# Weight-sum pieces of a decoder block: one event each, loaded and half summed through GpSimd, with six additions made by DMA

## The chip, the cores and the metric

The kernel runs on one core of a Trainium2 chip. A core has five engines with instruction queues of their own: TensorE (PE in the profile; its weight loads are listed as PEld), VectorE (DVE), ScalarE (ACT), GpSimd (POOL) and SyncE (SP, which here only issues DMAs). Each engine works through its queue in order; an instruction that must wait holds everything behind it on its engine. DMAs can be issued from SP, ACT and POOL, and run on 16 shared DMA engines. The metric is the time of the core in microseconds (us), a median over runs.

## The reference

One layer of a hybrid decoder block on x of 2048 tokens by 1024, everything in float32:

```python
h = _rmsnorm(x, norm_pre_mix)
proj = einsum('bsd,de->bse', h, w_in)            # q, k, v, u, z and two gates
merged = (gate_a * einsum('bse,ed->bsd', y_attn, w_branch_attn)
          + gate_b * einsum('bse,ed->bsd', y_gmlp, w_branch_gmlp))
y = einsum('bsd,de->bse', merged, w_out)
x = x + _rmsnorm(y, norm_post_mix)

h = _rmsnorm(x, norm_pre_mlp)
a = relu(einsum('bsd,df->bsf', h, w_mlp_in))     # 1024 -> 4096
y = einsum('bsf,fd->bsd', a * a, w_mlp_out)      # 4096 -> 1024
x = x + _rmsnorm(y, norm_post_mlp)
```

`y_attn` is a dilated window attention and `y_gmlp` a chunked spatial gating; both are done before the part of the kernel that is of interest here.

## The kernel before

**Precision.** A float32 operand is split into a high part (rounded to float32r) and a low part (the rest). A product of two such operands is three matmuls (high by high, high by low, low by high; `mm3`, lines 95 to 98). Each moves 512 columns. `split` (line 68) makes the two parts: a copy, usually on ACT, and a subtraction, usually on DVE (line 79).

**Fewer products.** The MLP's first product (w_mlp_in by h) is done with a two-level Strassen scheme in Winograd's form: seven outer products instead of eight, each of seven inner ones. The price is sums of operand blocks. For the outer level these are four sums of the weight blocks (S1 to S4) and four of the activation blocks (T1 to T4). They are worked out ahead, as *pieces*, and kept in DRAM (`ws_d` for the weights, `t_d` and `tq_d` for the activations).

**Part 2** is the stretch from the gated merge to x + norm(y). It goes over four chunks of 512 tokens in the order 2, 3, 0, 1. For each chunk:

- `merge` (line 1194) has eight turns `dt`, each with 18 matmuls. A turn needs two gates: `load_gate` (line 1182) loads them through SP into a few buffers, `open_gate` applies the sigmoid on ACT (line 1191), DVE multiplies them with the matmuls' result (line 1208), adds the two (line 1210), and `split` makes the operand `mg`.
- `out_block` (line 1232) has four blocks `i` of 128 tokens, each with 48 matmuls. Afterwards ACT squares the result out of PSUM for the norm (line 1256), DVE multiplies it by the gain (line 1257), adds the residual tile `xr` that SP has loaded (lines 1237 and 1261), POOL's queue stores it (`x1_d`, line 1264), and DVE makes the normed `y1` (line 1266). PE transposes `y1` later, in the middle of a later block or merge (line 1271, called through `flush`), and POOL's queue stores the transposed rows (`h2_d`, line 1273). There is one `xr` tile: SP reloads it once the store of the block before has read it.

**The pieces of Part 2.** `w_piece(t)` (line 1304) loads two slices of w_mlp_in of 512 KB, tile `v` (tag `tr`, `trw` in the profile) and tile `w` (tag `tq`, `tqw`), makes four sums of 128 x 512 in place, all on DVE (lines 1313 to 1317), and stores the two tiles through POOL's queue (lines 1315 and 1318). `t_piece` (line 1288) does the same with rows of h2. There is one buffer for each tile, so a piece's loads wait until the stores of the one before have landed. Both are generators with three steps; the loads are issued by SP. `next_piece` (line 1326) runs the next step whenever it is called: once in each of the last four turns of the first merge, once or twice after each output block of the first three chunks, and once in each turn of the later merges. There are 13 weight pieces (`W_EARLY`) and two activation pieces.

**Who sets the order.** PE's order is as written. In Part 2 the order of the other four engines is made by a planner, when the program is built: it takes the instruction whose inputs it expects to be ready. `behind` (line 179) pins what is issued inside it behind the last instruction issued so far on each engine; it sets the earliest place, not the place. From line 1748 on, in the MLP, `as_written` makes all engines follow the program.

**The MLP's first product** has 56 steps of seven inner products, 392 products of six matmuls, numbered `k`. The work beside them is put on a list with `later(k, ...)`. `combine` (line 1381) makes a step's weight sums: POOL adds, ACT rounds, DVE subtracts. `hproduct` (line 1538) adds the products into sums X by DVE (lines 1564 and 1566). For the outer product M5 (fourth of the seven), each result `t` is added to X, by POOL for column half 1 and by DVE for half 0 (line 1570, run from line 1957), and stored to `m5_d`. Two more kinds of pieces are on the list: `outer_load`, `outer_sum`, `outer_store` (from line 1494; eight pieces, one DVE and one POOL sum each, at k = 4 + 5n), and `w_load`, `w_sum`, `w_store` (from line 1515; the 16 - 13 = 3 late weight pieces, two DVE and two POOL sums each, at k = 118 + 6n). These two share the ring buffers `c1` and `xs`, four tiles each, and load and store through SP.

Of the kernel before, what the change touches and what calls it, by code (L numbers as in the profile page):

```python
# [9 lines left out]
F32 = mybir.dt.float32  # L10
F32R = mybir.dt.float32r
AF = mybir.ActivationFunctionType
OP = mybir.AluOpType
# [4 lines left out]
P = 128  # L18
# [3 lines left out]
NF = 32  # L22
# [3 lines left out]
HALF = 1024  # L26
# [16 lines left out]
def block_kernel(ctx, tc, a, out):  # L43
    nc = tc.nc
    pe, act, dve, pool, sp = nc.tensor, nc.scalar, nc.vector, nc.gpsimd, nc.sync
# [101 lines left out]
    h2_d = dtile([P, KT, S], "h2d")  # L147
# [221 lines left out]
    with ExitStack() as e1a:  # L369
# [12 lines left out]
        p = psum_aux("busy")  # L382
# [27 lines left out]
        with as_written():  # L410
# [5 lines left out]
            p = psum_aux("busy")  # L416
# [868 lines left out]

    T_AT, WS_AT = ("T1", "T3", "T4", "T2"), ("S2", "S4", "S3", "S1")

    def t_piece(kk):

        w, v = (ttp.tile([P, 2, 512], F32, name=f"{n}{kk}", tag=n, bufs=1) for n in ("tq", "tr"))  # L1290
        for t, k in ((w, kk), (v, kk + 2)):
            sp.dma_start(t.rearrange("p c t -> p (c t)"), h2_d[:, k, HALF:])
        yield
        b11, b12, b21, b22 = w[:, 0], w[:, 1], v[:, 0], v[:, 1]
        dve.tensor_sub(b11, b12, b11)
        dve.tensor_sub(b12, b22, b12)
        pool.dma_start(t_d[:, kk, 0:2], w)
        yield
        dve.tensor_sub(b22, b22, b11)
        dve.tensor_sub(b21, b21, b22)  # L1300
        pool.dma_start(t_d[:, kk, 2:4], v)
        yield

    def w_piece(t):

        w, v = (ttp.tile([P, 2, 512], F32, name=f"{n}w{t}", tag=n, bufs=1) for n in ("tq", "tr"))
        sp.dma_start(v.rearrange("p a c -> p (a c)"), a["w_mlp_in"][t + NF // 2].rearrange("p k c -> p (k c)"))
        yield
        sp.dma_start(w.rearrange("p a c -> p (a c)"), a["w_mlp_in"][t].rearrange("p k c -> p (k c)"))
        yield  # L1310
        a11, a12, a21, a22 = w[:, 0], w[:, 1], v[:, 0], v[:, 1]
        q, f = divmod(t, 2)
        dve.tensor_add(a22, a21, a22)
        dve.tensor_sub(a21, a11, a21)
        pool.dma_start(ws_d[q][:, 2:4, f], v)
        dve.tensor_sub(a11, a22, a11)
        dve.tensor_sub(a12, a12, a11)
        pool.dma_start(ws_d[q][:, 0:2, f], w)
        yield
# [6 lines left out]
    def next_piece(_=None):  # L1326
        while True:
            if not piece:
                if not pieces:
                    return  # L1330
                piece.append(pieces.popleft())
            with behind():
                try:
                    return next(piece[0])
                except StopIteration:
                    piece.clear()

    chunks = (2, 3, 0, 1)
    e3 = ExitStack()
# [146 lines left out]
    def later(k, f, *args):  # L1486
        todo.setdefault(k, []).append((f, args))
# [50 lines left out]
    def hproduct(k, n, i):  # L1538

        o, q = hsteps[n]  # L1540
        m = OUTER[o][0]
        j, name = USE[i]
        which = {1: "a", 6: "a", 7: "a", 4: "a", 2: "b", 5: "c", 3: "c"}[i]
        if i in (1, 2, 5):
            bank_[n, which] = psum_any(f"h{which}_{n}")
        p = bank_[n, which]
        for kk in range(2):
            w, b = hs_[n], w2_[(o, kk), name]
            for z, (l, r) in enumerate(((0, 0), (0, 1), (1, 0))):
                pe.matmul(p, w[:, l, S_AT[i], kk * P:(kk + 1) * P], b[r], start=i in (1, 2, 5) and not kk and not z,  # L1550
                          stop=kk == 1 and z == 2, skip_group_check=True)
        f, c = PLACE[i]
        first, last_one = i in (1, 6, 7, 4), i in (2, 3, 4, 5)
        x_ = X[2 * q + f][:, c * 512:(c + 1) * 512]
        if m in (2, 3, 5):
            if first:
                stage_[n, f, c] = rx.tile([P, 512], F32, name=f"e{n}{f}{c}", tag="c1" if c else "xs", bufs=4)
            t = stage_[n, f, c]
        else:
            t = x_  # L1560
        if m in (1, 5) and first:
            act.activation(t, p, AF.Copy)
        elif m in (2, 3) and first:
            dve.tensor_add(t, x_, p)
        else:
            dve.tensor_add(t, t, p)  # L1566
# [53 lines left out]
    def spatial_out(dt):  # L1620

        nonlocal ttp, gpost, gmlp
        if dt < 2:
            sz_out(*late.pop(0))
        if dt == 1:
            ez.close()
            mgp.append(stack(e2, "mg1", 1))
            gxp.append(stack(egx, "gx", 1))
            ttp = stack(e2r, "ttp", 2, side="right")
            load_wo(2)  # L1630
            load_wo(3)
        split_wo(dt)
        if dt > 3:
            next_piece()
# [12 lines left out]
    ttp = None  # L1647
# [2 lines left out]
    mg = merge(2, yt, {}, spatial_out)  # L1650
    for n, c in enumerate(chunks):
        if n:
            mg = merge(c, yt, {0: flush, 2: flush}, next_piece)
        for i in range(4):
            b = out_block(c, i, mg, flush_older)
            next(b)
            last.append(b)
            for _ in range((1, 2, 2, 0)[n]):
                next_piece()
# [31 lines left out]
    assert not pieces  # L1691

    def load_w2(q):

# [365 lines left out]
```

## Time and profile before

| | us |
|---|---|
| median of three runs (2649.35 to 2654.46) | 2650.83 |
| the profiled run | 2654.96 |
| its span in the profile | 2653.2 |
| PE busy in the span | 2567.0 |
| DVE busy | 1852.8 |
| POOL busy | 1364.0 |
| ACT busy | 1106.2 |

The page's fourth part gives a chain that covers almost nothing here, so the stages are read one by one. By the stretch view, the span's stages are: projections and attention from 0 to about 1010 us, the last gating chunks to 1062, Part 2 from 1062 to 1436, the first MLP product to 2026, and the second MLP product to the end. A matmul's own row shows 389 ns, but matmuls overlap: what counts is the distance from one start to the next, and so the number of matmuls in a stretch. "PEclk" is the granted clock of TensorE as a share of full speed.

### The profile page before, as it was taken

What the parts mean: (1) busy time and instruction counts of PE and PEld (TensorE: products, weight loads), DVE (VectorE), ACT (ScalarE), POOL (GpSimd) and SP (SyncE); (2) the same over time, 40 slices, a digit from 0 to 9 for tenths busy, and PEclk for the clock granted to TensorE, in tenths of its full rate; (3) what the DMA queues carried; (4) which work ended last, traced back from release to release, by engine and by line L of the source; (5) the groups of instructions that cost most, each with busy time, mean ns of one, the idle gap of its engine ahead of it and who ended that gap; (6) DMA issues with size and microseconds to landing.
All of it is one profiled execution on the core that took longest, in us unless ns stands there. A gap on an engine that the chain in (4) does not pass through costs nothing. (4 is left out here: it accounts for less than half of the span.)

```text
span 2653.2 us, 35700 instructions
## 1 busy us (share of the span) xinstructions
PE 2567.0 (97%) x12122; PEld 2127.6 (80%) x12122; DVE 1852.8 (70%) x3187; ACT 1106.2 (42%) x2324; POOL 1364.0 (51%) x1265
## 2 busy tenths in 40 slices
PE   9999999999999999989889999999999999999998
PEld 8888888788888877777667887877777888888886
DVE  5676665535443456766667889999888887788867
ACT  5213111254455444454435522443234555555555
POOL 0363354374454554211123656766698677677634
PEclk9999999999999999999999999999999999999999
DMA  8879768988888899866776467446885221222235
GB/s 320 285 245 327 261 229 289 300 278 255 291 288 236 234 304 318 287 213 230 243 251 228 166 190 230 139 159 194 249 250 175 89 81 62 88 88 88 88 115 210
DMA packets 412136, 568.69 MB, mean 214 GB/s; under 512 B 58801, under 2 KB 247473, under 8 KB 410930
## 3 DMA queue, kind: packets, MB, share of 16 engines
q1 hardware_dynamic: 385872, 502.63, 58.4%
q0 software_dynamic: 16192, 57.16, 5.5%
q10 hardware_dynamic: 9890, 6.62, 0.8%
q8 instruction: 96, 1.57, 0.2%
q14 instruction: 86, 0.70, 0.1%
HBM read 362.16 MB, written 204.14 MB: 213 GB/s over the span
## 5 line engine op out<-in xcount | busy, mean ns | idle before, releaser
L1550 PE MATMUL ha<-spot,hs 128*128 128x512 f32 x1344 | 334.9, 396 | 27.5 <-DVE X_yt L1566 10.4
L1550 PEld LDWEIGHTS ha<-spot,hs 128*128 128x128 f32 x1344 | 252.1, 190 | 92.3 <-DVE X_yt L1566 10.7
L1859 PE MATMUL ya<-spot,s 128*128 128x512 f32 x1344 | 323.5, 389 | 2.3 <-DVE X_yt L1867 2.3
L1859 PEld LDWEIGHTS ya<-spot,s 128*128 128x128 f32 x1344 | 252.2, 188 | 55.3 <-issue 1.8
L1550 PE MATMUL hc<-spot,hs 128*128 128x512 f32 x672 | 173.7, 394 | 2.8 <-DVE e L1566 1.8
L728 PE MATMUL g<-opA,spots 128*128 128x512 f32 x672 | 170.8, 398 | 1.9 <-DVE cv L760 1.9
L1859 PE MATMUL yc<-spot,s 128*128 128x512 f32 x672 | 170.5, 389 | 0.0
L728 PE MATMUL g<-opB,spots 128*128 128x512 f32 x648 | 164.7, 398 | 0.3 <-DVE ga L766 0.3
L1550 PEld LDWEIGHTS hc<-spot,hs 128*128 128x128 f32 x672 | 127.3, 191 | 33.1 <-DVE e L1566 3.5
L96 PE MATMUL x<-hT_a,wq 128*128 128x512 f32 x384 | 149.7, 390 | 0.0
L98 PE MATMUL x<-hT_a,wq 128*128 128x512 f32 x384 | 149.4, 389 | 0.0
L97 PE MATMUL x<-hT_a,wq 128*128 128x512 f32 x384 | 149.4, 389 | 0.0
L1859 PEld LDWEIGHTS yc<-spot,s 128*128 128x128 f32 x672 | 126.2, 188 | 26.2
L728 PEld LDWEIGHTS g<-opA,spots 128*128 128x128 f32 x672 | 120.9, 188 | 24.2 <-issue 2.3
L79 POOL TENSOR_TENSOR spots<-gr,spots 128x512 fp32r<-128x512 f32 x98 | 127.9, 1309 | 23.7 <-DMA gr<-in_w_in_dram 9.4
L1723 ACT ACTIVATE sraw<-sraw 128x1024 f32<-128x1024 f32 x128 | 134.7, 1052 | 1.7
L79 POOL TENSOR_TENSOR spot<-w2r,spot 128x512 fp32r<-128x512 f32 x79 | 112.1, 1443 | 45.1 <-ACT spot L71 45.1
L728 PEld LDWEIGHTS g<-opB,spots 128*128 128x128 f32 x648 | 116.6, 188 | 22.3 <-POOL spots L73 0.7
L71 ACT ACTIVATE hl<-r 128x512 fp32r<-128x512 f32 x48 | 30.4, 633 | 236.5 <-POOL r L329 89.0
L978 DVE TENSOR_REDUCE o<-po 128x256 f32<-128x512 f32 x48 | 33.2, 692 | 132.1 <-PE po L977 132.1
L73 POOL TENSOR_SCALAR spots<-gr 128x512 fp32r<-128x512 f32 x86 | 55.4, 645 | 134.6 <-PE g L728 92.0
L96 PE MATMUL o<-wo,mg 128*128 128x512 f32 x256 | 101.9, 398 | 2.1 <-ACT mg L71 2.1
(460 smaller groups left out, 6801.6 us busy)
## 6 DMA issues: line engine op xcount, KB each, us to landing
sraw<-sd SPq DMA_DIRECT2D x128, 256.0 KB, 3.3
qk<-hl SPq DMA_DIRECT2D x24, 1024.0 KB, 5.7
qq<-qk SPq DMA_DIRECT2D x96, 256.0 KB, 5.3
sd<-e SPq DMA_DIRECT2D x64, 256.0 KB, 4.9
hraw<-wsd SPq DMA_DIRECT2D x32, 512.0 KB, 4.6
w2r<-in_w_mlp_out_dram SPq DMA_DIRECT2D x16, 1024.0 KB, 8.2
g<-gated SPq DMA_DIRECT2D x56, 256.0 KB, 5.9
gr<-sgd SPq DMA_DIRECT2D x53, 256.0 KB, 5.2
```

Of the source, the lines that this page charges most:

```text
L71: act.activation(hi, src, AF.Copy)
L73: pool.tensor_scalar(hi, src, 1.0, 1.0, op0=OP.mult, op1=OP.mult)
L79: (pool if lo_eng == "pool" else dve).tensor_sub(lo, src, f32(hi))
L96: pe.matmul(ps, lh, rh, start=start, stop=False)
L97: pe.matmul(ps, lh, rl, start=False, stop=False)
L98: pe.matmul(ps, ll, rh, start=False, stop=stop)
L728: pe.matmul(p, w[:, l, k], h[:, r, k], start=i in (1, 6, 5, 4) and not k and not m, stop=k == 3 and m == 2, skip_group_check=True)
L978: dve.tensor_reduce(ot[:, :, j * 64:(j + 1) * 64], po.rearrange("p (b h e) -> p b e h", b=4, h=2), axis=AX.X, op=OP.add)
L1550: pe.matmul(p, w[:, l, S_AT[i], kk * P:(kk + 1) * P], b[r], start=i in (1, 2, 5) and not kk and not z, stop=kk == 1 and z == 2, skip_group ...
L1723: act.activation(sraw_[n], sraw_[n], func)
L1859: pe.matmul(p, s[:, l], w[r], start=i in (1, 2, 5) and not m and not o, stop=m == 1 and o == 2, skip_group_check=True)
```

## The change

It has three parts.

1. In Part 2 a piece takes one event. `next_piece(c, kind, i)` acts only at places named in a table: at turn `i` of chunk `c`'s merge (`"m"`) or after its output block `i` (`"b"`). An event first finishes the piece that is open (sums and stores), then starts the next (both loads). The loads are issued by POOL's queue instead of SP. Of the four sums two stay on DVE and two go to POOL. There are 14 weight pieces instead of 13, so 16 pieces, at 17 events; the last merge has four of them.
2. In the first MLP product two late weight pieces are left instead of three. They begin at k = 38 and 43 instead of 118, 124 and 130. The eight activation pieces follow each other every 4 products instead of 5.
3. For M5, in the last three of its eight steps, the six additions of column half 1 are made by a DMA from POOL's queue that adds to its target, instead of by a POOL instruction.

```diff
     def t_piece(kk):
-        w, v = (ttp.tile([P, 2, 512], F32, name=f"{n}{kk}", tag=n, bufs=1) for n in ("tq", "tr"))
+        w, v = pair(kk)
         for t, k in ((w, kk), (v, kk + 2)):
-            sp.dma_start(t.rearrange("p c t -> p (c t)"), h2_d[:, k, HALF:])
+            pool.dma_start(t.rearrange("p c t -> p (c t)"), h2_d[:, k, HALF:])
         yield
...
     def w_piece(t):
-        w, v = (ttp.tile([P, 2, 512], F32, name=f"{n}w{t}", tag=n, bufs=1) for n in ("tq", "tr"))
-        sp.dma_start(v.rearrange("p a c -> p (a c)"), a["w_mlp_in"][t + NF // 2].rearrange("p k c -> p (k c)"))
-        yield
-        sp.dma_start(w.rearrange("p a c -> p (a c)"), a["w_mlp_in"][t].rearrange("p k c -> p (k c)"))
+        w, v = pair(f"w{t}")
+        for z, n in ((v, t + NF // 2), (w, t)):
+            pool.dma_start(z.rearrange("p a c -> p (a c)"), a["w_mlp_in"][n].rearrange("p k c -> p (k c)"))
         yield
         a11, a12, a21, a22 = w[:, 0], w[:, 1], v[:, 0], v[:, 1]
         q, f = divmod(t, 2)
         dve.tensor_add(a22, a21, a22)
         dve.tensor_sub(a21, a11, a21)
         pool.dma_start(ws_d[q][:, 2:4, f], v)
-        dve.tensor_sub(a11, a22, a11)
-        dve.tensor_sub(a12, a12, a11)
+        pool.tensor_sub(a11, a22, a11)
+        pool.tensor_sub(a12, a12, a11)
         pool.dma_start(ws_d[q][:, 0:2, f], w)
-        yield
-    W_EARLY = 13
-    pieces = deque([w_piece(t) for t in range(W_EARLY - 2)] + [t_piece(0), t_piece(1)] +
-                   [w_piece(t) for t in range(W_EARLY - 2, W_EARLY)])
+    W_EARLY = 14
+    pieces = deque([w_piece(t) for t in range(10)] + [t_piece(0), t_piece(1)] + [w_piece(t) for t in range(10, W_EARLY)])
+    PIECE_AT = {(2, "m"): (5,), (2, "b"): (0, 1, 3), (3, "m"): (2, 6), (3, "b"): (1, 3), (0, "m"): (2, 6), (0, "b"): (1, 3),
+                (1, "m"): (1, 3, 5, 7), (1, "b"): (0,)}
+    def next_piece(c, kind, i):
+        if i not in PIECE_AT[c, kind]:
+            return
+        with behind():
+            if piece:
+                next(piece.pop(), None)
+            if pieces:
                 piece.append(pieces.popleft())
+                next(piece[0])
...
         if m == 5:
-            later(k + 1, (pool if c else dve).tensor_add, x_, x_, t)
+            if c and q > 4:
+                later(k + 1, collect, x_, t)
+            else:
+                later(k + 1, (pool if c else dve).tensor_add, x_, x_, t)
             later(k + 3, sp.dma_start, m5_d[q][:, 2 * f + c], t)
             return
+    def collect(to, t):
+        pool.dma_start(to, t, accum_op=OP.add)
...
     for n in range(8):
-        t = 4 + 5 * n
+        t = 4 + 4 * n
...
     for n in range(NF // 2 - W_EARLY):
-        t = 7 * 2 * HQ + 6 + 6 * n
+        t = 38 + 5 * n
```

The remaining lines of the diff put `next_piece`'s new arguments at the places that call it.

More of the change, by code (lines that the diff above doesn't have):

```diff
@@ L1286, in block_kernel, with pair @@
     T_AT, WS_AT = ("T1", "T3", "T4", "T2"), ("S2", "S4", "S3", "S1")
+    def pair(name):
+        return [ttp.tile([P, 2, 512], F32, name=f"{n}{name}", tag=n, bufs=1) for n in ("tq", "tr")]
     def t_piece(kk):
-        w, v = (ttp.tile([P, 2, 512], F32, name=f"{n}{kk}", tag=n, bufs=1) for n in ("tq", "tr"))
+        w, v = pair(kk)
         for t, k in ((w, kk), (v, kk + 2)):
-            sp.dma_start(t.rearrange("p c t -> p (c t)"), h2_d[:, k, HALF:])
+            pool.dma_start(t.rearrange("p c t -> p (c t)"), h2_d[:, k, HALF:])
         yield
@@ L1297, in t_piece @@
         pool.dma_start(t_d[:, kk, 0:2], w)
-        yield
-        dve.tensor_sub(b22, b22, b11)
-        dve.tensor_sub(b21, b21, b22)
+        pool.tensor_sub(b22, b22, b11)
+        pool.tensor_sub(b21, b21, b22)
         pool.dma_start(t_d[:, kk, 2:4], v)
-        yield
     def w_piece(t):
-        w, v = (ttp.tile([P, 2, 512], F32, name=f"{n}w{t}", tag=n, bufs=1) for n in ("tq", "tr"))
-        sp.dma_start(v.rearrange("p a c -> p (a c)"), a["w_mlp_in"][t + NF // 2].rearrange("p k c -> p (k c)"))
-        yield
-        sp.dma_start(w.rearrange("p a c -> p (a c)"), a["w_mlp_in"][t].rearrange("p k c -> p (k c)"))
+        w, v = pair(f"w{t}")
+        for z, n in ((v, t + NF // 2), (w, t)):
+            pool.dma_start(z.rearrange("p a c -> p (a c)"), a["w_mlp_in"][n].rearrange("p k c -> p (k c)"))
         yield
@@ L1315, in w_piece @@
         pool.dma_start(ws_d[q][:, 2:4, f], v)
-        dve.tensor_sub(a11, a22, a11)
-        dve.tensor_sub(a12, a12, a11)
+        pool.tensor_sub(a11, a22, a11)
+        pool.tensor_sub(a12, a12, a11)
         pool.dma_start(ws_d[q][:, 0:2, f], w)
-        yield
-    W_EARLY = 13
-    pieces = deque([w_piece(t) for t in range(W_EARLY - 2)] + [t_piece(0), t_piece(1)] +
-                   [w_piece(t) for t in range(W_EARLY - 2, W_EARLY)])
+    W_EARLY = 14
+    pieces = deque([w_piece(t) for t in range(10)] + [t_piece(0), t_piece(1)] + [w_piece(t) for t in range(10, W_EARLY)])
     piece = []
[L1326 to L1330, printed above, removed]
-                piece.append(pieces.popleft())
[L1332 to L1336, printed above, removed]
+    PIECE_AT = {(2, "m"): (5,), (2, "b"): (0, 1, 3), (3, "m"): (2, 6), (3, "b"): (1, 3), (0, "m"): (2, 6), (0, "b"): (1, 3),
[7 more added lines that the diff above has]
+            if pieces:
+                piece.append(pieces.popleft())
+                next(piece[0])
     chunks = (2, 3, 0, 1)
@@ L1632, in spatial_out @@
         split_wo(dt)
-        if dt > 3:
-            next_piece()
+        next_piece(2, "m", dt)
         if dt == KT - 1:
@@ L1652, in block_kernel @@
         if n:
-            mg = merge(c, yt, {0: flush, 2: flush}, next_piece)
+            mg = merge(c, yt, {0: flush, 2: flush}, lambda dt: next_piece(c, "m", dt))
         for i in range(4):
@@ L1657, in block_kernel @@
             last.append(b)
-            for _ in range((1, 2, 2, 0)[n]):
-                next_piece()
+            next_piece(c, "b", i)
             if n < 3 and not i:
@@ L1690, in block_kernel @@
                     first_split(2, kk)
-    assert not pieces
+    assert not pieces and not piece
     def load_w2(q):
```

## The prediction

> **What bounds the kernel now.** I read the page's first part, then the stretch view cut by stage (merge and output blocks 1062 to 1436 us, "Part 2"; first MLP product 1436 to 2026; second to the end) and in 25 us slices. Columns: us, then busy us (x instructions) of PE, PEld, DVE, ACT, POOL, then granted clock, DMA share, GB/s.
>
> ```profile
> PE 2567.0 (97%) x12122; PEld 2127.6 (80%) x12122; DVE 1852.8 (70%) x3187; ACT 1106.2 (42%) x2324; POOL 1364.0 (51%) x1265
> 1062.00:1436.00 374.00, 340.60 (x1520) 277.21 (x1519) 247.65 (x480) 164.30 (x307) 68.82 (x94) 0.96 0.68 235
> 1436.00:2026.00 590.00, 558.34 (x2392) 448.59 (x2392) 527.02 (x699) 219.40 (x405) 413.80 (x369) 0.99 0.64 204
> 1125.00:1150.00 25.00, 20.12 (x85) 16.57 (x84) 10.32 (x30) 16.70 (x30) 1.97 (x4) 0.86 0.43 151
> 1275.00:1300.00 25.00, 20.34 (x80) 16.27 (x79) 16.80 (x27) 8.42 (x15) 2.85 (x4) 0.86 0.78 263
> 1375.00:1400.00 25.00, 23.44 (x93) 18.39 (x94) 18.01 (x29) 7.29 (x12) 2.86 (x4) 0.93 0.66 219
> 1500.00:1525.00 25.00, 24.50 (x108) 19.95 (x108) 24.00 (x32) 15.82 (x31) 15.10 (x14) 1.00 0.20 68
> 1525.00:1550.00 25.00, 25.00 (x112) 20.70 (x111) 21.74 (x33) 4.93 (x9) 10.15 (x13) 1.00 0.80 253
> 1600.00:1650.00 50.00, 43.77 (x177) 33.97 (x176) 46.70 (x60) 10.94 (x20) 34.36 (x31) 0.95 0.78 263
> 1750.00:1775.00 25.00, 21.16 (x86) 16.66 (x84) 24.70 (x32) 13.49 (x26) 16.83 (x13) 0.93 0.39 126
> ```
>
> PE is the bound. An undisturbed slice holds 112 matmuls, 0.223 us each. Part 2 leaves PE idle for 374 - 340.6 = 33 us, and its worst slices run at a clock of 0.86, which costs 0.14 x 25 = 3.5 us more each. The first MLP product leaves it idle for 32 us; there DVE works 89% of the time, in Part 2 only 66%. So DVE is short of throughput in the MLP, while in Part 2 something makes it late. The waits of Part 2 (engine, line, what it waited for: us in total, times, longest) say what:
>
> ```profile
> SPq L1307 <- DMA wsd<-trw: 43.1, 10, 6.9
> SPq L1309 <- DMA wsd<-tqw: 15.7, 9, 4.6
> SPq L1237 <- DMA x1d<-xr: 105.4, 13, 14.1
> SPq L1182 <- DVE g L1210: 31.4, 9, 8.9
> ACT g L1191 <- DMA g<-gated: 78.6, 33, 6.4
> DVE trw L1313 <- DMA trw<-in_w_mlp_in_dram: 14.8, 4, 5.7
> DVE trw L1314 <- DMA tqw<-in_w_mlp_in_dram: 4.5, 3, 1.8
> ```
>
> SP stands 59 us in front of piece loads until the previous piece's store has landed; the gate loads queue behind them, and ACT waits 79 us for gates. DVE itself stands 19 us for piece loads. The order in time at the largest stalls, the idle time in brackets:
>
> ```profile
> 1123.26 0.33 SPq L1307 DMA_DIRECT2D trw<-in_w_mlp_in_dram  x1
> 1124.89 2.14 SPq L1182 DMA_DIRECT2D g<-gated  x4
> 1127.81 0.63 ACT L1191 ACTIVATE g<-g 128x512 f32<-128x512 f32 x1 [4.56 <-DMA g<-gated]
> 1129.08 1.29 DVE L1257 TENSOR_TENSOR y<-o,gpost 128x512 f32<-128x512 f32 x2 [5.47 <-ACT junk L1256]
> 1142.44 0.87 PE L1271 MATMUL pt<-ident,y 128*128 128x128 f32 x3 [4.88 <-DVE y L1266]
> ...
> 1280.29 0.69 DVE L1313 TENSOR_TENSOR trw<-trw 128x512 f32<-128x512 f32 x1 [3.98 <-DMA trw<-in_w_mlp_in_dram]
> 1281.64 0.80 PE L96 MATMUL b<-yt,wb 128*128 128x512 f32 x1 [4.66 <-DVE g L1208]
> ...
> 1374.22 0.69 DVE L1313 TENSOR_TENSOR trw<-trw 128x512 f32<-128x512 f32 x1 [5.71 <-DMA trw<-in_w_mlp_in_dram]
> 1375.57 0.80 PE L96 MATMUL b<-yt,wb 128*128 128x512 f32 x1 [4.80 <-DVE g L1208]
> ```
>
> First: a piece load holds SP, gates come late, ACT stands in a sigmoid, the squares behind it are late, then DVE, then PE. Second and third: DVE stands directly for a piece load, and the matmuls wait for their bank.
>
> **The change, part 1: pieces in Part 2.** Moving the loads off SP removes its 59 us of waits. Giving a piece one event, with sums at the next, leaves 11 to 22 us between load and sums in the first three chunks (output blocks are 48 matmuls, 10.7 us; four merge turns of 18 are 16 us). Prices:
>
> ```profile
> L1316 DVE TENSOR_TENSOR tqw<-trw,tqw 128x512 f32<-128x512 f32 x13 | 8.9, 688 | 0.1
> L1526 POOL TENSOR_TENSOR wt<-wt,wt 128x512 f32<-128x512 f32 x3 | 3.9, 1296 | 8.5 <-DVE wt L1524 8.5
> L1318 POOL DMA_DIRECT2D wsd<-tqw x13 | 9.4, 723 | 20.4 <-DVE tqw L1317 18.7 <-DVE t_post L113 1.7
> wsd<-tqw POOLq DMA_DIRECT2D x13, 512.0 KB, 5.0
> tqw<-in_w_mlp_in_dram SPq DMA_DIRECT2D x13, 512.0 KB, 5.5
> ```
>
> Before, 15 pieces x 4 sums = 60 on DVE. After, 16 x 2 = 32 on DVE and 32 on POOL: DVE loses 28 x 0.69 = 19 us, POOL gains 32 x 1.30 = 42 us and 32 load issues at 0.72 = 23 us. POOL is busy 69 us of 374, so the room is there. What is queued behind POOL's new waits (a load waits for a store, 5.0 us) are the x1 and h2 stores; SP waits for the x1 store before it reloads xr (the 105 us row). I cost that at nothing where a piece is done before its block's x1 store, 2 us if not.
>
> What PE gets back: the stall at 1142 (4.9 + 3.5 of clock = 8.4) and at 1281 (4.7 + 3.5 = 8.2) are the pieces' doing: 16.6. Gates and xr come late for other reasons too (31 and 105 us), so I take three quarters, 12.5. Four shorter waits follow gate loads held up the same way or a DVE that is behind, 7.1 us in all; the first and the last of the four:
>
> ```profile
> 1192.36 0.50 PE L96 MATMUL b<-yt,wb 128*128 128x512 f32 x1 [1.96 <-DVE g L1208]
> 1324.42 0.84 PE L1271 MATMUL pt<-ident,y 128*128 128x128 f32 x6 [2.11 <-DVE y L1266]
> ```
>
> Half of them, 3.5. The last merge now gets four pieces instead of two, so its 4.8 isn't credited, and I charge 2 for the additional piece and the locks below. Part 1: **-14 us**; bounds -28 (all of it, the last merge too) and +13 (third rival).
>
> **Part 2: the first MLP product.** One late weight piece fewer, and the other two start at product 38 instead of 118.
>
> ```profile
> L1524 DVE TENSOR_TENSOR wt<-wt,wt 128x512 f32<-128x512 f32 x3 | 2.1, 688 | 0.4 <-DMA wt<-in_w_mlp_in_dram 0.3
> L1528 DVE TENSOR_TENSOR wt<-wt,wt 128x512 f32<-128x512 f32 x3 | 3.3, 1098 | 0.2 <-POOL wt L1526 0.2
> wt<-in_w_mlp_in_dram SPq DMA_DIRECT2D x12, 256.0 KB, 6.4
> ```
>
> In 1600 to 1650 PE makes 177 matmuls of 224: 47 x 0.223 = 10.5 us lost. The pieces there cost DVE 5.4 of its 46.7 us and POOL 8. I credit half, 5. The new place, product 38 on, is near 1436 + 38 x 1.34 = 1487; DVE is at 24.0 of 25 in 1500 to 1525 and gets 2 x 1.8 us more. The loads take the buffers of the last outer pieces, so SP waits for a store, and 6.4 us of landing is longer than the four products (5.4 us) to the first sum: DVE may stand 1 to 3 us in its order. The outer pieces, every 4 products, move about two sums ahead of it. Cost 4. Net **-1**, between -6 and +6.
>
> **Part 3: six additions by DMA** (M5, last three steps of that pass).
>
> ```profile
> 1763.84 1.64 POOL L1957 TENSOR_TENSOR X_gpost<-X_gpost,e 128x512 f32<-128x512 f32 x1 [3.04 <-DVE e L1566]
> 1764.28 1.75 DVE L1957 TENSOR_TENSOR X_xr<-X_xr,e 128x512 f32<-128x512 f32 x1
> 1766.68 0.50 PE L1550 MATMUL ha<-spot,hs 128*128 128x512 f32 x1 [3.69 <-DVE e L1564]
> ```
>
> The DVE addition takes 1.75 instead of 0.68 because POOL's runs: it ends 0.68 us after POOL has finished. PE then waits 3.7. An issue of 0.72 takes the place of 1.64. No trace shows an accumulating DMA; its sum is next read 56 products (75 us) later, so landing times from 5 us up cost nothing, and the bounds are 0 and the 5.8 us that 1750 to 1775 loses (26 matmuls). I take **-2**, nearer to the one stall seen.
>
> **Sum:** -14 - 1 - 2 = -17 us. From the profiled run, 2654.96 (span 2653.2), that is 2638; from the median of the three runs, 2650.83, which is the number to beat, **2634**.
>
> **The rivals.** (a) *Gates stay late*: SP's freed time is taken by its waits for gate buffers (31 us) and for x1 stores (105 us). Then 1142 and the shorter waits stay, and of part 1 only 1281's 8.2 less 2 remains: -6 - 3 = -9, 2642. For it: ACT's gate waits are 33, SP's waits for stores 19. Against: at 1123 the order is plain.
>
> (b) *POOL's sums block DVE.* In the pair above the DVE row lost 1.07 us to a POOL row. If each of the 32 does that, DVE loses 34 us and saves 19; 15 us more, most of it ending in PE's waits, leaves 17 - 13 = 4: 2647, no change. Against: DVE idles a third of Part 2, and matrix evictions read one operand from PSUM. The Trainium skill, SBUF — State Buffer, "Who interferes with whom", states this rule: a DVE instruction with two SBUF inputs and a GpSimd instruction that reads SBUF exclude each other, and whichever starts later blocks. By that rule, which the 1.75 us row bears out, this rival's lock is real and only its frequency is open.
>
> (c) *Slower: the last merge.* A piece's chain is 0.69 (DVE) + 2 x 1.30 (POOL) + 5.0 (store lands) + 5.5 (load lands) = 13.8 us, and with issues 14.5. Events there are two turns apart, 36 matmuls, 8.0 us. Four pieces fall behind by 6.5 us each. If DVE's order puts the sums at their events, it stands there; the rows above turn a DVE wait of 4.0 and 5.7 into 4.7 and 4.8 of PE. At 6 us and 2.5 of clock each, 34 us, less the 6.5 lost there now: +27 - 17 = +10, 2661. It outweighs the gain from some 4 us of DVE wait per piece. For it: two of the pieces before stood so. Against: the planner orders engines by expected readiness, so late sums are placed late; `behind` sets only the earliest place.
>
> **How the numbers follow.** Forecast 0.58, (a) 0.14, (b) 0.14, (c) 0.14. Faster by over 0.2% (5.3 us, about what a measurement tells from no change): the forecast and (a), 0.72; same: (b), 0.14; slower: (c), 0.14. The range runs from 2617 (both upper credits) to 2657, leaving out most of (c).
>
> **What would show it.** Right: no SP wait on piece stores in Part 2, ACT's wait for gates well under 79 us, the slices at 1142 and 1281 at clock 1.00, Part 2 near 360 us. 1600 to 1650 above 190 matmuls, and a new dip near 1500 of at most 4 us. Wrong: DVE waits of 4 us and more for piece loads in the last merge (c); two-operand DVE rows of Part 2 well above 0.69 us (b); gate waits as before with SP waiting for buffers (a).

## The result, and the profile after

| | before | after |
|---|---|---|
| median, us (range) | 2650.89 (2649.35 to 2654.46) | 2671.69 (2667.88 to 2677.87) |
| ratio, 95% interval | | 1.0079, 1.0057 to 1.01 |
| span of the profiled run, us | 2653.2 | 2670.5 |

The change made the kernel slower by 0.8%, above the predicted range. A single execution can lie several us from its kernel's median, and the stages below are read from one profiled execution each: the one of before took 2654.96 us, 4 above its median here and 7 to 9 above the medians of before that were taken beside the experiments (2646.15 to 2648.27). e6's profiled execution took 8289 us, so its stages are not given. Where the time went is seen first from the first starts of four kinds of matmul, in the view of single tiles (the times behind the colon are the ns of one, then the first and last start in us). Before, then after:

```profile
L96 PE MATMUL b<-yt,wb x192: 389/389/795, 1062.7 to 1387.3; 128*128 128x512 f32 x192
L1550 PE MATMUL ha<-spot,hs x1344: 387/389/794, 1436.9 to 2024.3; 128*128 128x512 f32 x192
L1550 PE MATMUL hb<-spot,hs x336: 387/389/542, 1440.5 to 2008.1; 128*128 128x512 f32 x168
L1859 PE MATMUL ya<-spot,s x1344: 387/389/496, 2013.2 to 2558.7; 128*128 128x512 f32 x192
```

```profile
L96 PE MATMUL b<-yt,wb x192: 389/389/796, 1060.8 to 1387.6; 128*128 128x512 f32 x192
L1548 PE MATMUL ha<-spot,hs x1344: 387/389/797, 1447.6 to 2041.1; 128*128 128x512 f32 x192
L1548 PE MATMUL hb<-spot,hs x336: 387/389/628, 1458.4 to 2024.9; 128*128 128x512 f32 x168
L1861 PE MATMUL ya<-spot,s x1344: 387/389/500, 2030.0 to 2575.5; 128*128 128x512 f32 x192
```

From the first `b` to the first `ha` is Part 2: 374.2 us before, 386.8 after. From `ha` to `hb`, two neighbouring products, is the MLP's start: 3.6 and 10.8. From `hb` to the first `ya` is the rest of the first MLP product: 572.7 and 571.6. So +12.6, +7.2 and -1.1: the loss is in Part 2 and at its end. The order in time has the first matmul of the last chunk's output blocks, before and after:

```profile
1388.99 0.47 PE L96 MATMUL o<-wo,mg 128*128 128x512 f32 x1 [0.82 <-ACT mg L71]
```

```profile
1388.32 0.39 PE L96 MATMUL o<-wo,mg 128*128 128x512 f32 x1
```

Up to there Part 2 took 326.3 and 327.5 us: no loss. The last blocks took 48.0 and 59.3. Last blocks and start together, the **seam**, grew from 51.5 to 70.1: +18.6, nearly all of it. But up to the last blocks nothing was gained either, where 14 us had been forecast. The stretch view of after, columns as in the prediction:

```profile
1062.00:1436.00 374.00, 336.42 (x1481) 271.64 (x1480) 238.48 (x425) 142.33 (x277) 117.23 (x143) 0.95 0.66 227
1125.00:1150.00 25.00, 25.00 (x120) 20.88 (x119) 17.43 (x35) 6.26 (x16) 11.11 (x13) 1.00 0.60 211
1275.00:1300.00 25.00, 21.04 (x88) 15.81 (x86) 14.22 (x20) 7.25 (x12) 6.23 (x7) 1.00 0.78 275
1525.00:1550.00 25.00, 18.78 (x72) 14.76 (x71) 23.68 (x30) 11.92 (x24) 16.11 (x14) 0.86 0.36 127
1600.00:1650.00 50.00, 47.45 (x207) 38.31 (x206) 45.33 (x61) 17.09 (x31) 29.83 (x29) 1.00 0.58 174
1768.00:1793.00 25.00, 22.61 (x98) 17.71 (x96) 24.86 (x34) 13.85 (x27) 15.46 (x16) 1.00 0.68 180
```

From the first `hb` on, the work comes 18 us later than before (1458.4 and 1440.5), so the last line is the work that 1750 to 1775 held before. The stall of 1142 is gone: its slice went from 85 matmuls at a clock of 0.86 to 120 at 1.00. But the same 374 us hold 39 matmuls fewer, with POOL busier by 48 us. The waits of Part 2 after the change (us in total, times, longest):

```profile
SPq L1237 <- DMA x1d<-xr: 164.5, 11, 33.9
ACT g L1191 <- DMA g<-gated: 60.2, 27, 4.9
POOL tqw L1309 <- DMA wsd<-tqw: 25.7, 11, 4.9
POOL trw L1309 <- DMA wsd<-trw: 6.0, 3, 3.8
DVE trw L1313 <- DMA trw<-in_w_mlp_in_dram: 23.7, 8, 4.9
DVE trw L1314 <- DMA tqw<-in_w_mlp_in_dram: 14.8, 6, 4.0
DVE xr L1261 <- DMA xr<-in_x_dram: 23.1, 6, 6.8
```

SP's 59 us of waits for piece stores are gone, and ACT's waits for gates fell from 79 to 60. But DVE now stands 38.5 us for piece loads (19.3 before), and POOL stands 32 us for piece stores. The order in time shows a piece's round at the end of the last merge, from sums to sums:

```profile
1391.93 0.69 DVE L1313 TENSOR_TENSOR trw<-trw 128x512 f32<-128x512 f32 x1 [4.23 <-DMA trw<-in_w_mlp_in_dram]
1393.13 0.68 DVE L1314 TENSOR_TENSOR trw<-tqw,trw 128x512 f32<-128x512 f32 x1
1394.27 0.73 POOL L1315 DMA_DIRECT2D wsd<-trw  x1 [6.96 <-DVE trw L1314]
1395.01 1.30 POOL L1316 TENSOR_TENSOR tqw<-trw,tqw 128x512 f32<-128x512 f32 x1
1395.05 1.82 DVE L1210 TENSOR_TENSOR g<-g,g 128x512 f32<-128x512 f32 x1
1396.39 1.64 POOL L1317 TENSOR_TENSOR tqw<-tqw 128x512 f32<-128x512 f32 x1
1398.34 0.76 POOL L1318 DMA_DIRECT2D wsd<-tqw  x1 [0.31 <-POOL tqw L1317]
1399.10 0.57 POOL L1309 DMA_DIRECT2D trw<-in_w_mlp_in_dram  x1
1401.88 0.55 POOL L1309 DMA_DIRECT2D tqw<-in_w_mlp_in_dram  x1 [2.21 <-DMA wsd<-tqw]
1403.72 0.69 DVE L1313 TENSOR_TENSOR trw<-trw 128x512 f32<-128x512 f32 x1 [4.54 <-DMA trw<-in_w_mlp_in_dram]
1406.48 0.69 DVE L1314 TENSOR_TENSOR trw<-tqw,trw 128x512 f32<-128x512 f32 x1 [2.07 <-DMA tqw<-in_w_mlp_in_dram]
```

The second sum comes again after 13.35 us (1393.13 to 1406.48): sums by POOL, store issued, store landed, load issued, load landed, all one behind the other, because the next load goes into the tile that the last store reads. DVE stands 4.54 and 2.07 us in it. And beside POOL's first sum, DVE's addition of two gates (line 1210) takes 1.82 us. Its group over Part 2, before and after:

```profile
L1210 DVE TENSOR_TENSOR g<-g,g 128x512 f32<-128x512 f32 x27 | 18.6, 689 | 0.5
```

```profile
L1210 DVE TENSOR_TENSOR g<-g,g 128x512 f32<-128x512 f32 x27 | 26.9, 998 | 0.6
```

So POOL's sums have two ways to cost: the **lock** (DVE's two-operand instructions held up) and the **round** of a piece made longer. The seam is a matter of its own.

### The profile page after: what moved, and what is told of

The parts are those of the page before. It is cut to its first block, busy times and chain, and to the rows that moved or that the text cites. A ratio compares the mean times of both kernels' runs of the same rounds, so it can differ in the third digit from the quotient of the medians.

```text
span 2670.5 us, 35646 instructions
## 1 busy us (share of the span) xinstructions
PE 2571.0 (96%) x12122; PEld 2129.0 (80%) x12122; DVE 1863.0 (70%) x3157; ACT 1097.1 (41%) x2316; POOL 1419.6 (53%) x1329
```

## The experiments

All stage times are of one profiled run each, read as above; an edit also lets the planner place other work anew. The rest, whose program is the same in the change, e3, e4 and e9 to e13, lies between 566.0 and 573.2 there. So a stage difference of up to some 7 us is a hint, and the ratios of the whole time decide. "Up to" is Part 2 up to the last blocks, so Part 2 is the first two columns together; the seam is "last blocks" and "start"; "rest" is `hb` to `ya`. Ratios are to the kernel before, on the same chip, with the 95% interval.

| run | median | ratio | up to | last blocks | start | rest |
|---|---|---|---|---|---|---|
| before | | | 326.3 | 48.0 | 3.6 | 572.7 |
| the change | 2671.69 | 1.0079 (1.0057 to 1.01) | 327.5 | 59.3 | 10.8 | 571.6 |
| e1: part 1 only | 2668.71 | 1.0086 (1.0064 to 1.0108) | 326.5 | 59.4 | 10.8 | 570.9 |
| e2: parts 2, 3 only | 2645.73 | 1.0 (0.9987 to 1.0014) | 319.2 | 51.5 | 3.5 | 566.7 |
| e3: loads by SP | 2659.54 | 1.0055 (1.0036 to 1.0075) | 321.4 | 54.6 | 10.5 | 571.1 |
| e4: sums by DVE | 2642.93 | 0.9986 (0.9974 to 0.9998) | 306.7 | 52.3 | 15.0 | 569.9 |
| e5: last merge less | 2662.15 | 1.0059 (1.0036 to 1.0081) | 323.5 | 54.7 | 3.5 | 580.2 |
| e6: e5 with e4 | 2640.83 | 0.9977 (0.9962 to 0.9992) | | | | |
| e9: e4, reads by POOL | 2671.48 | 1.0101 (1.0073 to 1.0129) | 320.7 | 67.5 | 11.0 | 569.7 |
| e10: e4, memsets | 2647.74 | 1.0 (0.9987 to 1.0013) | 309.0 | 56.2 | 11.7 | 571.4 |
| e11: e4, half the reads | 2652.38 | 1.002 (1.0009 to 1.003) | 313.2 | 54.4 | 11.5 | 572.8 |
| e12: e4, longer round | 2679.2 | 1.0125 (1.0109 to 1.0141) | 315.4 | 80.4 | 12.1 | 566.0 |
| e13: e4, spread | 2646.75 | 1.0 (0.9989 to 1.0011) | 317.1 | 47.8 | 3.5 | 573.2 |
| e14: e4, three tiles | 2634.44 | 0.9946 (0.9932 to 0.996) | 300.4 | 46.3 | 10.3 | 571.0 |
| e15: change, three tiles | 2640.81 | 0.9968 (0.9955 to 0.9981) | 309.4 | 45.3 | 12.5 | 568.7 |
| e16: e14, spread | 2627.66 | 0.9924 (0.9911 to 0.9937) | 302.9 | 46.3 | 3.5 | 568.7 |

**Which part.** e1 has the change's Part 2 and the old lists in the MLP; e2 the old steps of the pieces (with 14 weight pieces) and the new lists.

```diff
-        t = 4 + 4 * n        # e1, on the change
+        t = 4 + 5 * n
...
-        t = 38 + 5 * n
+        t = 7 * 2 * HQ + 6 + 6 * n
...
-            if c and q > 4:
+            if False:
```

> The new pieces of Part 2 (14 of them) with the MLP lists of before: activation pieces every 5 products, the two late weight pieces at 118 and 124, all M5 additions on POOL. If the pieces of Part 2 carry the loss, the distance from the first merge matmul to the first MLP matmul stays near 387 us (374 before) and the time is 2666 to 2675. If the MLP's new lists carry it, that distance is unchanged too but the first MLP product is shorter by 6 us and more and the time is near 2655.

> Pieces of Part 2 as before (three steps, loads by SP, sums by DVE), only 14 weight pieces instead of 13 so that two are left; the MLP lists of the change. If Part 2 carries the loss: 2645 to 2653, the first MLP product about 573 to 578 us long (576 before). If the MLP lists carry it: 2665 and more, the product near 590 us.

e1 has the whole loss, in the same stages; e2 equals the kernel before in its time. So part 1 is the cause. (From `b` to `ya` the profile of e2 is 9.7 us shorter than that of before, though the two kernels take the same time: against before's profile a gain can come out too large, and a loss too small, by up to that much.)

**Which edit of part 1.** e3 issues the loads by SP again, e4 gives all sums to DVE again:

```diff
-            pool.dma_start(t.rearrange("p c t -> p (c t)"), h2_d[:, k, HALF:])
+            sp.dma_start(t.rearrange("p c t -> p (c t)"), h2_d[:, k, HALF:])      # e3, and w_piece's loads alike
```

```diff
-        pool.tensor_sub(a11, a22, a11)
-        pool.tensor_sub(a12, a12, a11)
+        dve.tensor_sub(a11, a22, a11)
+        dve.tensor_sub(a12, a12, a11)      # e4, and t_piece's alike
```

> The change, but the piece loads are issued by SP again. If POOL's queue, standing for store landings in front of loads, delays the x1 stores and so xr and DVE, Part 2 comes back to about 376 us and the time to about 2658. If it is the chain of a piece against four pieces in the last merge, or the port lock, nothing comes back: 2668 to 2680, with SP waiting 50 us and more for piece stores again.

> The change, but all four sums of a Part 2 piece on DVE. If the lock between DVE and POOL carries the loss, the gate additions return from 1.00 to 0.69 us each and the time falls by 8 to 14 us, to 2658 to 2664. If it is the chain in the last merge, a piece's chain is only about 1 us shorter, four pieces give back about 5 us, 2664 to 2670, and the first MLP matmul still comes 6 us and more after that of before.

e4 brings Part 2 to 359.1 us and is a little faster than the kernel before (0.14%). Up to the last blocks it takes 306.7: what remains of part 1 gains 19.6 there against the profile of before and 12.5 against e2's (319.2), and POOL's sums cost 20.8 (327.5 less 306.7). They don't explain the seam, 67.3 in e4. By the ratios POOL's sums cost 0.93% of the time (1.0079 less 0.9986), some 25 us. e3 brings 6.1 us back up to the last blocks and 4.7 in them, although SP waits for stores again; by the ratios that is 0.24%, with intervals that overlap (the waits of SP's queue in e3):

```profile
SPq L1237 <- DMA x1d<-xr: 64.3, 12, 14.4
SPq L1309 <- DMA wsd<-trw: 48.7, 10, 7.8
SPq L1309 <- DMA wsd<-tqw: 40.8, 12, 5.9
```

There POOL's queue no longer stands for piece stores, and SP's longest wait for an x1 store falls from 33.9 to 14.4. That this is where e3 gains is likely and not shown apart. The start stays at 10 to 15 in both: another cause.

**The seam.** e5 ends the pieces at turn 5 of the last merge and leaves two more for the MLP; e6 does that with all sums on DVE.

```diff
-    W_EARLY = 14
+    W_EARLY = 12
...
-                (1, "m"): (1, 3, 5, 7), (1, "b"): (0,)}
+                (1, "m"): (1, 3, 5), (1, "b"): ()}
...
-        t = 38 + 5 * n
+        t = (38, 43, 118, 124)[n]
```

> The change with the pieces of the last merge ended early: 12 weight pieces in Part 2 instead of 14, the last finished at turn 5 of the last merge (the events at its turn 7 and after its first output block go), and four late pieces in the MLP, at products 38, 43, 118 and 124. The half sums by POOL stay. Theory: the 10.8 us between the first two MLP products (3.6 before) come from the last pieces' stores, which hold the buffers of the MLP's first weight load; with them done some 25 us earlier that stretch is back at 3 to 5 us, the last output blocks gain 2 to 3, and two pieces more in the MLP cost 2 to 3: some 2663 us. Rival: the start of the MLP is late for another reason (POOL or DVE busy with the MLP's own first sums); then it stays at 9 us or more and the time at 2672 or above.

> The run before with all four sums of a piece on DVE. If the two losses (POOL's sums and the last merge's pieces) add up, Part 2 is 355 to 360 us, the MLP's start 3 to 5, and the time some 2633 us (2628 to 2639), faster than both kernels. Rival: DVE, not the stores, sets the last merge's end, or the two additional late pieces cost the MLP what they save: 2641 to 2645, as with all sums on DVE alone.

The start is back at 3.5 us and the last blocks lose 4.6 less, so the late last pieces make 11.9 of the seam's 18.6. The MLP's first weights go into the memory that the pieces held, behind the last store; their first load, by the time order of the change and of the kernel before:

```profile
1440.06 0.73 POOL L1318 DMA_DIRECT2D wsd<-tqw  x1 [0.41 <-POOL tqw L1317]
1442.13 0.38 SPq L1377 DMA_DIRECT2D hraw<-in_w_mlp_in_dram  x1
```

```profile
1394.17 0.94 SPq L1379 DMA_DIRECT2D hraw<-in_w_mlp_in_dram  x1
```

That is 5.5 us ahead of the first product (1447.6) instead of 42.7. But two late pieces more made the MLP's rest 8.6 us longer (580.2 against 571.6), 4.3 a piece, where 2 to 3 for both had been expected; so e6 gains little over e4.

**Lock or round.** e9 adds to e4 reads of POOL that lie beside the store's landing; e10 was to make the round longer without reads.

```diff
+    def beside(w, v):      # e9: after both stores of a piece
+        e = ttp.tile([P, 128], F32, name="beside", tag="beside", bufs=1)
+        for c0 in range(0, 1024, 128):
+            pool.tensor_sub(e, w[:, c0 // 512, c0 % 512:c0 % 512 + 128], v[:, c0 // 512, c0 % 512:c0 % 512 + 128])
```

```diff
+    def beside(z):      # e10: ahead of a piece's last store
+        e = ttp.tile([P, 128], F32, name="beside", tag="beside", bufs=1)
+        pool.tensor_sub(e, z[:, 0, :P], z[:, 1, :P])
+        for _ in range(11):
+            pool.memset(e, 0.0)
```

> All sums on DVE, and after both stores of a piece are issued POOL makes eight subtractions of 128x128 that read the two tiles and write a spare one: as many elements read as the two sums that POOL had, but outside of the chain sums, stores, next loads (they run while the stores land). Theory lock: what cost 28 us is that POOL's reads of SBUF hold up DVE's additions of two SBUF operands; then Part 2 grows from 359 us to 373 or more, the gates' additions take 0.9 us or more, and the time is 2656 or above. Theory chain: it was the longer way from a piece's sums to its stores and to the next loads; then Part 2 stays at 363 or less, even where some additions are longer, and the time at 2645 or so.

> All sums on DVE, and before a piece's last store POOL makes one subtraction of 128x128 and eleven memsets of 128x128 (0.25 us each, some 3 us together): the chain is as long as with POOL's two sums, but POOL hardly reads SBUF. Theory chain: Part 2 grows from 359 us to 373 or more, with the gates' additions still at 0.69 us. Theory lock: Part 2 stays at 363 or less.

Neither told them apart. e9's eight subtractions took some 0.62 us each, 5.0 for a piece, and held the loads behind them on POOL; the gates' additions grew only to 738 ns. In e10 the store didn't depend on the memsets and went ahead of most of them. e11 and e12 mend both: four subtractions instead of eight, and a last POOL instruction that the store must wait for.

```diff
-        for c0 in range(0, 1024, 128):      # e11, on e9
+        for c0 in range(0, 1024, 256):
...
+        pool.tensor_add(z[:, 0, :1], z[:, 0, :1], e[:, :1])      # e12, on e10, at the end of beside
```

> As the run with eight subtractions beside, but with four of 128x128 for each piece: those eight took 5 us of POOL for each piece, longer than a store's landing (3.8 us), and so held the loads behind them; four take 2.4 us, about as long as POOL's two sums in the change (2.6 us), and end before the store has landed. Theory lock (POOL's reads beside DVE's additions are the cost): Part 2 is 373 us or more (359 with all sums on DVE), DVE's two-operand rows are 10 us longer in all, the time 2656 or above. Theory chain (the loads held up behind POOL's work): Part 2 at 365 or less, the time at 2650 or less, as in the run with memsets.

> The run with memsets, mended: there the last store didn't depend on them and was issued ahead of most of them. Now POOL ends with adding the zero to one column of the tile, so the last store of a piece waits some 3.3 us for POOL as in the change, with hardly a read of SBUF. Theory chain: the way from the sums to the next piece's loads is what cost; Part 2 at 373 or more and DVE's waits for piece loads above 40 us, the time 2656 or above. Theory lock: Part 2 at 367 or less, the time at 2651 or less.

e12 has the longer round and hardly a read, and lost 36.6 us of Part 2 over e4, with the gates' additions at their old length: 8.7 up to the last blocks and 28.1 in them, where the pieces, further and further behind, hold up the MLP's first load. Its rows:

```profile
L1210 DVE TENSOR_TENSOR g<-g,g 128x512 f32<-128x512 f32 x27 | 18.6, 688 | 0.4
POOL tqw L1317 <- DMA wsd<-tqw: 51.6, 12, 7.4
DVE trw L1321 <- DMA trw<-in_w_mlp_in_dram: 31.8, 9, 8.1
DVE trw L1322 <- DMA tqw<-in_w_mlp_in_dram: 10.3, 7, 4.2
DVE xr L1261 <- DMA xr<-in_x_dram: 32.7, 8, 7.1
```

POOL stands twice as long for the stores as in the change, and DVE 42 us for piece loads and 33 for `xr`, whose reload waits for an x1 store queued behind POOL's waits (31 and 19 in e4). e12 met what the round's theory had expected. e11, reads with nearly e4's round, lost 6.5 us up to the last blocks and 2.1 in them; by the ratios that is 0.34% (9 us). Its Part 2, 367.6 us, and its time fell between the two theories. So up to the last blocks the longer round alone cost 8.7 and the reads alone 6.5, both near what one profile can tell, and neither is the change's own price. e12's rounds are longer than the change's: in the last merge the second sum comes again after 15.0 to 21.4 us, after 13.3 to 14.4 in the change and after 11.1 to 11.7 in e4. And e11's reads meet DVE less often: the gates' additions took 732 ns, 998 in the change.

An estimate of all that is held takes the five groups of DVE with two SBUF inputs that got longer up to the last blocks (the gates' additions, the two subtractions of `split`, and lines 109 and 114 of the norm), and multiplies their counts with what their means are above e4's. It gives some 20 us in the change, 4 in e11 and none in e12. So both the lock and the round cost time; their sizes in the change don't follow from these two runs. The seam became much longer where the round did (e12's last blocks).

**The round made shorter.** Three tiles in rotation instead of two: a piece's first load finds a free tile, the second waits for the *first* store of the piece before, which POOL's sums don't delay. One of the two tiles of transposed rows is given up for it (and two of the raw w_out slices change their tile).

```diff
-        return [ttp.tile([P, 2, 512], F32, name=f"{n}{name}", tag=n, bufs=1) for n in ("tq", "tr")]
+        return [ttp.tile([P, D], F32, name=f"{n}{name}", tag="tp", bufs=3).rearrange("p (a c) -> p a c", a=2)
+                for n in ("tq", "tr")]
...
-        w, v = pair(f"w{t}")
+        v, w = pair(f"w{t}")
...
-            ttp.tile([P, D], F32, name=f"tt{c}{i}", tag="tt")
+            ttp.tile([P, D], F32, name=f"tt{c}{i}", tag="tt", bufs=1)
```

> All sums on DVE, and the two tiles of a piece taken from three in rotation (one of the two tiles of the transposed rows is given up for it): the first load of a piece finds a free tile, the second waits only for the first store of the piece before. Theory chain: the way from sums to the next sums is 1.5 to 3 us shorter, DVE's waits for piece loads fall from 31 us to below 20, Part 2 from 359 to some 352 (348 to 357), the time to some 2634. Rival (the way no longer matters once DVE makes the sums, or the single tile of transposed rows costs as much): Part 2 at 358 or more.

> The change, its POOL sums kept, with three tiles in rotation: now neither of the next loads waits for a store that comes after POOL's sums. Theory chain: most of the 28 us of POOL's sums come back, since they are out of the way: Part 2 at 362 to 370 (386.8 in the change), the rest, some 8 us, being POOL's reads beside DVE; the gates' additions still near 0.95 us; the time 2648 to 2656. Theory lock: the additions stay long and so does the time: Part 2 at 380 or more, 2664 or above.

e15 is the change with its POOL sums kept and only its tiles changed: up to the last blocks it fell from 327.5 to 309.4 us, the last blocks from 59.3 to 45.3, and the kernel is faster than before by 0.3%. Part 2 came to 354.7 us, below the 362 to 370 that were expected. Its round and its waits (the names are swapped by the edit: `tqw` is the tile loaded and stored first):

```profile
1387.99 0.73 POOL L1317 DMA_DIRECT2D wsd<-tqw  x1 [2.47 <-DVE tqw L1316]
1388.74 1.30 POOL L1318 TENSOR_TENSOR trw<-tqw,trw 128x512 f32<-128x512 f32 x1
1390.12 1.29 POOL L1319 TENSOR_TENSOR trw<-trw 128x512 f32<-128x512 f32 x1
1391.72 0.76 POOL L1320 DMA_DIRECT2D wsd<-trw  x1 [0.31 <-POOL trw L1319]
1392.48 0.57 POOL L1311 DMA_DIRECT2D trw<-in_w_mlp_in_dram  x1
```

```profile
DVE tqw L1316 <- DMA trw<-in_w_mlp_in_dram: 15.3, 6, 5.0
L1211 DVE TENSOR_TENSOR g<-g,g 128x512 f32<-128x512 f32 x27 | 20.4, 755 | 0.6
L109 DVE SCALAR_TENSOR_TENSOR t_post<-r_post,v_post 128x1 f32<-128x1 f32 x12 | 6.8, 571 | 0.4
```

The load at 1392.48 is issued right behind the last store's issue (1391.72), without a wait. DVE's waits for weight-piece loads are 15 us instead of 38.5. The gates' additions were expected to stay near 0.95 us and fell to 755 ns: POOL's sums meet them less often there. But they hold the norm's small instructions as long as in the change (line 109: 571 ns in e15, 566 in the change, 219 in e4), and by the estimate above, against e14, some 15 us of DVE are held in e15, 20 in the change. So three quarters of the lock are still there, and POOL's sums cost much less: up to the last blocks 9.0 us with three tiles (309.4 against e14's 300.4) and 20.8 with two, and by the ratios of the whole time 0.22% (0.9968 less 0.9946, some 6 us) instead of 0.93%. Up to the last blocks some 12 us go with the long round, what it adds in collisions included.

**Spread.** e13 keeps all pieces in Part 2 but ends them earlier, by three events in the second and third merges; e16 does that with three tiles.

```diff
-    PIECE_AT = {(2, "m"): (5,), (2, "b"): (0, 1, 3), (3, "m"): (2, 6), (3, "b"): (1, 3), (0, "m"): (2, 6), (0, "b"): (1, 3),
-                (1, "m"): (1, 3, 5, 7), (1, "b"): (0,)}
+    PIECE_AT = {(2, "m"): (5,), (2, "b"): (0, 1, 3), (3, "m"): (1, 4, 7), (3, "b"): (1, 3), (0, "m"): (1, 4, 7),
+                (0, "b"): (1, 3), (1, "m"): (1, 3, 5), (1, "b"): ()}
```

> All sums on DVE, all 16 pieces kept in Part 2, but one event more in each of the second and third merges (at turns 1, 4 and 7) and the last piece finished at turn 5 of the last merge instead of after its first output block; the two activation pieces come two places later. Theory: what is left of the loss, 11 us at the MLP's start, comes from the last pieces being late, and two late pieces instead of four cost the MLP nothing more: Part 2 356 to 362, the start 3 to 6, the time some 2633 us (2628 to 2639), faster than both kernels. Rival: three events in a merge are too near to each other there (10.7 to 12 us for a piece whose way takes 11 to 14): Part 2 at 367 or more and the time at 2643 or more.

> All sums on DVE, three tiles in rotation, and the events spread as before (three in the second and third merges, the last piece done at turn 5 of the last merge). If the way no longer binds, spreading costs nothing and the MLP starts 3 to 6 us after its first product instead of 15: Part 2 352 to 358, the time some 2627 us (2621 to 2634). Rival: Part 2 at 363 or more as with two tiles, the time 2643 or more.

With two tiles the seam is mended (51.3 instead of 67.3), but the nearer events cost 10.4 us up to the last blocks, and the time, 2646.75 us, equals that of before, where some 2633 had been expected. With three tiles they cost 2.5, the seam is 6.8 shorter than in e14, and the time met the 2627 that were expected. e16 is the best version found, 2627.66 us: 0.76% faster than the kernel before and about 1.5% faster than the change (0.9924 over 1.0079).

## Why the prediction was wrong

The forecast was -17 us; up to the first `ya` the change lost 18.7 (969.2 from `b` to `ya`, 950.5 before). Term by term:

| term | forecast | measured | from |
|---|---|---|---|
| events, loads off SP (14 and the 2 charged) | -16 | -19.6 | up to the last blocks, e4 less before |
| locks, one more piece | +2 | +20.8 | up to the last blocks, change less e4 |
| the seam | 0 | +18.6 | change less before |
| lists and M5 in the MLP | -3 | -1.1 | rest, change less before |

The first term held in sign and, as far as single profiles can tell, in size (19.6 against the profile of before, 12.5 against e2's): SP's waits for piece stores went, the slices at 1142 and 1281 run at a clock of 1.00, and Part 2 came to 359.1 in e4 where the prediction said near 360. The last can't be told from nothing: e2 has it without part 1, and equals before within 0.14% (3.7 us). Its pieces were mis-sized: 1600 to 1650 makes 207 matmuls (above 190, as said), the work of 1750 to 1775 makes 98 instead of 86, and the new dip, at 1525 to 1550, is 40 matmuls deep, 8.9 us where "at most 4" was said.

**The first step that failed** is the charge of "2 for the additional piece and the locks". The prediction had the round right, 14.5 us from rows (13.35 measured above), but compared it with the events only in the last merge. For the first three chunks it looked at the "11 to 22 us between load and sums" and took the round as covered. e12 and e15 show that it wasn't: the round alone made longer than in the change cost 8.7 us ahead of the last blocks, made shorter (with three quarters of the lock still there) it gave back 18.1 there. So the charge of 2 measured +20.8, of which some 12 go with the long round (20.8 less the 9.0 of three tiles), collisions that it adds included. How the round reaches PE is read from the waits and not shown by a run of its own. The prediction named two stands. DVE at the head of its queue for a load it costed only in the last merge, in rival (c); DVE stands 38.5 us in the change, 31 in e4 and 15 in e15. POOL at the head of its queue for a store, in front of the x1 stores that SP's reload of `xr` waits for, it costed at 2 or nothing; e3, without that stand, is 0.24% faster than the change, some 6 us, but e4 is faster still with 42 us of such stands.

**The second** is a term that was missing: what the last pieces hold. The prediction followed the last merge's four pieces to DVE, not to the memory that the MLP's first load needs. e5, e13 and e16 bring the start back to 3.5 us by ending the pieces earlier.

**Rival (b)**, the lock, was real, and one of two shares. The Trainium skill, SBUF — State Buffer, "Who interferes with whom", states that a DVE instruction with two SBUF inputs and a GpSimd instruction that reads SBUF exclude each other, while a DVE instruction with at most one SBUF input, outside the 2-port modes, doesn't contend. The traces agree with both halves: additions of two SBUF tiles went from 689 to 998 ns, and the products that read PSUM stayed (681 ns before, 679 after):

```profile
L1208 DVE TENSOR_TENSOR g<-g,b 128x512 f32<-128x512 f32 x56 | 37.9, 679 | 0.0
```

Its price up to the last blocks is 6.5 us by e11 less e4, where some 4 us of DVE are held, and at most 9.0 by e15 less e14, where 15 are held. In the change 20 are held; in proportion to e15 that is up to 12 us, an estimate. The rival had priced it at 13, and alone would have ended at "no change". How the lock and the round add isn't settled to better than that. One reading beside this rival was off without harm to it: in the prediction's pair of rows DVE ends 0.55 us after POOL (1766.03 and 1765.48), not 0.68.

**Rival (c)** had the sign and the mechanism, a round too long for the last merge, at 2661. Its place was wrong: the last merge took 44.0 us, less than before (46.4, from the starts of its first matmul and of the last blocks). The pieces that fell behind were paid for behind it, in the last blocks and the start.

**Rival (a)** is not what happened: gate waits fell from 79 to 60, and e4, with 53, got the gain up to the last blocks that had been forecast.

Open: why DVE stands for loads even where events are 16 us and more apart. That the planner puts the sums where it expects the load, too early, would fit; it wasn't tried. Of the seam's 18.6 us, e5 explains 11.9; the other 6.7 in the last blocks are not split between lock and round.

## What to carry to other kernels

Work that goes through one set of buffers is a closed round: add up the way from its sums through store, landing, next load and landing back to the sums, and compare it with the spacing of the events everywhere, not only where it looks tight. Moving an operation to an idle engine is not free if it lies in that round; a third tile in rotation shortened it, and Part 2 by 32 us with it (386.8 to 354.7). And see where the last round ends: the next stage's first load may need its memory.

## What was not expected of the hardware

The lock holds up even instructions of one column, and for as long as POOL's runs. At the seam of the change:

```profile
1436.98 1.30 POOL L1316 TENSOR_TENSOR tqw<-trw,tqw 128x512 f32<-128x512 f32 x1
1437.07 1.23 DVE L109 SCALAR_TENSOR_TENSOR t_post<-r_post,v_post 128x1 f32<-128x1 f32 x1
1438.36 1.29 POOL L1317 TENSOR_TENSOR tqw<-tqw 128x512 f32<-128x512 f32 x1
1438.53 1.14 DVE L114 TENSOR_TENSOR r_post<-r_post,t_post 128x1 f32<-128x1 f32 x1
```

The two small DVE instructions of the norm take 1.23 and 1.14 us, where the same lines took 0.22 and 0.15 us at 1429.94 and 1431.62 with no sum of POOL beside them, and each ends within 0.02 us of POOL's. Both have two inputs in SBUF. The norm's one-input instruction between them (line 113) isn't held: over Part 2 up to the last blocks its mean is 154 ns in the change and in e4, while from e4 to the change line 109 goes from 219 to 566 ns and line 114 from 159 to 483 (the rows of `t_post` and `r_post`). These two lines, 24 short instructions, make 8 of the 20 us that DVE is held.
